# A decoder layer on one core: the 24 gate columns move from strips beside the first projection into the value projection

## The chip, the cores and the metric

The kernel runs on one NeuronCore of a Trainium2 chip. The metric is the device time of one execution in microseconds (us), the median over the runs. One execution is profiled as well; all rows below are of that execution. The core has a matrix engine (TensorE, PE in the rows, with its weight loads as PEld), a vector engine (DVE), a scalar engine (ACT), GpSimd (POOL) and queues for transfers (DMA), which SyncE (SP) issues.

## The reference

One decoder layer over 512 tokens of width 1024, everything in float32. A single input projection makes all the operands of two token mixers, among them three gates for each of eight attention heads, 24 columns in all:

```
h = x @ w_in + b_in
(q_a, kv_a, g_nsa, z_a, q_b, f_b, i_b, z_b, gm_a, gm_b) = split(h)
gates = sigmoid(g_nsa)          # 8 heads x 3 branches = 24 columns
o_a = gates[0]*o_cmp + gates[1]*o_slc + gates[2]*o_win
o_b = hgrn2(q_b, f_b, i_b); o_b = o_b * rsqrt(mean(o_b^2)+eps) * g
y = sigmoid(gm_a)*((o_a*silu(z_a)) @ Wa) + sigmoid(gm_b)*((o_b*silu(z_b)) @ Wb)
out = layer_norm(alpha*x + y @ w_out)
```

Mixer A is sparse attention with a compressed, a selected and a window branch; mixer B is a gated linear recurrence in chunks of 64 tokens.

## The kernel before

Every float32 operand of a large product is split into a high part in a reduced format and the rest (`split2`: a cast on ACT, then a subtraction on DVE), and a product is three matmuls: high by high, high by low, low by high. The input is held transposed, as eight tiles of 128 channels by 512 tokens (`xh[kt]`, `xl[kt]`, `kt` from 0 to 7).

The PE's work is one long list in program order, and so are the transfers that SP issues. First comes the projection to the forget gates `f`, a loop over `kt` in which each step does 12 matmuls into four PSUM tiles (pools `pso` and `pss`). At `kt` 3 and 7 this loop also does the gates: four unsplit float32 matmuls each, with 32 columns of weights `wgs`, whose results go to the four strips of 32 partitions of one tile `gps` (pool `pst`). ACT copies it with the bias to the tile `graw`: channels lie in partitions there, tokens along the row, and the four strips are partial sums.

Then come the projections to `q` of mixer B, the four token blocks of `proj_i` (tokens in partitions, 512 columns, 24 matmuls a block), each closed by a DVE addition of the bias (line 275), and a sequence of weight tiles of 1024 columns, which `load` brings in and `split` splits two tiles ahead. Between them a cooperative scheduler (`weave`) places pieces of other work at fixed points: it starts generators, each of which does a piece at every tick. The gates are one of these, `gates()`, started ahead of the third block of `proj_i`: four transposes of `graw` on PE, a DVE sum over the four strips, and the sigmoid with an Exp on ACT and three small DVE steps, on a tile `gat` of 128 by 128.

`proj_v` is the projection to the values, with tokens in partitions and 256 columns. Its two weight tiles `v0` and `v1` hold four `kt` each, one token block takes 24 matmuls, and after each block DVE adds the bias (line 295), ACT casts and DVE subtracts into `vv`. Behind it on PE stand the sums of squares for the norm of mixer B (`hgrn_norm`, eight records with the operand `ones`). The norm goes on through DVE line 431, ACT lines 435 and 436, sixteen small transfers on SP, and POOL line 448. Tiles of one pool share its buffers in turn, so a new tile waits for the last reader of the one that had its place before: three buffers each for the weight tiles `wraw`, `whi`, `wlo`, 67 for the general pool `t2`.

Of the kernel before, what the change touches and what calls it, by code (L numbers as in the profile page):

```python
# [18 lines left out]
P = 128  # L19
KT = DM // P  # L20
# [17 lines left out]
           "ga0 gb0 ga1 gb1 ga2 gb2 ga3 gb3 ga4 gb4 ga5 gb5 ga6 gb6 ga7 gb7").split()  # L38
M_INDEX = {n: i for i, n in enumerate(M_TILES)}
NB = 4 + len(M_TILES)  # L40


BRANCH = [("b", 0), ("b", 2), ("a", 0), ("b", 4), ("a", 2), ("b", 6), ("a", 4), ("a", 6)]
# [12 lines left out]
O_NG = O_LB + 8  # L56
O_PEK = O_NG + 4
O_PEV = O_PEK + 16
O_GB = O_PEV + 16
O_END = O_GB + 1  # L60


K_ID, K_TRI, K_CM, K_RV, K_SM, K_COS, K_SIN, K_MASK, K_END = (
# [29 lines left out]


@with_exitstack
def layer_kernel(ctx: ExitStack, tc: tile.TileContext, xT, xn, w0, wi, wg, wf, small, brow, consts,
                 w1, w2, wbr, wout, lng, lnb, out):
    nc = tc.nc
    V, A, G = nc.vector, nc.scalar, nc.gpsimd
# [10 lines left out]
    def dma(o, i):  # L110
        tc.keep_in_program_order(nc.sync.dma_start(o, i))  # L111
# [10 lines left out]
    def T2(n=512, dt=F32):  # L122
        return t2.tile([P, n], dt, name="t2", tag="t2")
# [10 lines left out]
    def PT():  # L134
        return pst.tile([P, 512], F32, name="pst", tag="pst")
# [10 lines left out]
    def split2(src, dst_hi, dst_lo):  # L146
        A.copy(dst_hi, src)  # L147
        V.tensor_tensor(dst_lo, src, dst_hi.bitcast(F32), ALU.subtract)  # L148
# [10 lines left out]
        T.matmul(warm[:, 0:128], zero, zero, start=True, stop=True)  # L159
    sml = cst.tile([P, O_END], F32, name="sml")  # L160
    con = cst.tile([P, K_SM], F32, name="con")
    wgs = T2(256)
    xs, xh, xl = [], [], []
    fps = [PO(), PO(), PS(), PS()]
    gps = PT()
    for kt in range(KT):
        xr, wr = first if kt == 0 else (T2(), T2())
        dma(xr, xT[:, kt])
        if kt:
            dma(wr, w0[kt])  # L170
        if kt == 1:
            dma(wgs, wg)
        if kt == 4:
            dma(sml, small)
        h, l, wh, wl = T2(dt=F32R), T2(dt=F32R), T2(dt=F32R), T2(dt=F32R)
        xh.append(h)
        xl.append(l)
        A.copy(h, xr)
        V.tensor_copy(wh, wr)
        V.tensor_tensor(l, xr, h.bitcast(F32), ALU.subtract)  # L180
        V.tensor_tensor(wl, wr, wh.bitcast(F32), ALU.subtract)
        xs.append(xr)
        for a, b in ((wh, h), (wh, l), (wl, h)):
            for m in range(4):
                T.matmul(fps[m], a[:, 128 * m:128 * m + 128], b, start=kt == 0 and a is wh and b is h,
                         stop=kt == KT - 1 and a is wl)
        if kt == 3 or kt == 7:
            for k in range(kt - 3, kt + 1):
                q = k % 4
                T.matmul(gps[32 * q:32 * q + 32], wgs[:, 32 * k:32 * k + 32], xs[k], start=k < 4, stop=k >= 4)  # L190


    order = M_TILES + ["br%s%d" % b for b in BRANCH]
# [27 lines left out]

    ones = cst.tile([P, 32], F32, name="ones")
    G.memset(ones, 1.0 / 128.0)
    epst = cst.tile([P, 1], F32, name="epst")
    G.memset(epst, EPS)
    hbias = cst.tile([P, NB], F32, name="hbias")
    V.tensor_scalar(hbias, sml[:, 0:NB], 0.5, None, ALU.mult)
    attn_sb = [T2() for _ in range(4)]
    for t in attn_sb:
# [6 lines left out]
    G.memset(kcB, 0.0)  # L236
    G.memset(vcB, 0.0)
    split(0)
    graw = T2()
    A.activation(graw, gps, AF.Identity, bias=sml[:, O_GB:O_GB + 1])  # L240
    sig_f = []
    for m in range(4):
        s = T2()
# [21 lines left out]
    def proj_i(tt):  # L265
# [9 lines left out]
        tc.keep_in_program_order(V.tensor_tensor(v, ps, bri, ALU.add))  # L275
        vi.append(v)

    def proj_v():
        i = M_INDEX["v0"]
        load(i + 3)  # L280
        split(i + 2)
        load(i + 4)
        for tt in range(4):
            c = slice(128 * tt, 128 * tt + 128)
            ps = PA()
            for kt in range(KT):
                if kt % 4 == 0:
                    weave.tick()
                hi, lo = parts[i + kt // 4]
                n = slice(256 * (kt % 4), 256 * (kt % 4) + 256)  # L290
                T.matmul(ps[:, 0:256], xh[kt][:, c], hi[:, n], start=kt == 0, stop=False)
                T.matmul(ps[:, 0:256], xh[kt][:, c], lo[:, n], start=False, stop=False)
                T.matmul(ps[:, 0:256], xl[kt][:, c], hi[:, n], start=False, stop=kt == KT - 1)
            v = T2(256)
            tc.keep_in_program_order(V.tensor_tensor(v, ps[:, 0:256], brv, ALU.add))
            vd = vv[:, tt].rearrange("p b (g c) -> p b g c", c=64)
            v4 = v.rearrange("p (b g c) -> p b g c", b=2, c=64)
            split2(v4, vd[:, :, 0:4:3], vd[:, :, 1:3])
            vts.append(vv[:, tt])
        split(i + 3)  # L300

    def silu_tile(name):
# [211 lines left out]
                    A.copy(dst, ps[r:r + 32, 0:64])  # L514
        ready.add("cmp")

    gat = cst.tile([P, 4, 32], F32, name="gat")
    gv = gat[:, :, 0:24].rearrange("p i (h b) -> p i h b", b=3)

    def gates():  # L520
        ps = transpose4(graw)
        gflat = gat.rearrange("p i c -> p (i c)")
        tc.keep_in_program_order(
            V.tensor_reduce(gat, ps.rearrange("p (i q c) -> p i c q", i=4, q=4), AX.X, ALU.add))
        A.activation(gflat, gflat, AF.Exp, scale=-1.0)
        V.tensor_scalar(gflat, gflat, 1.0, 2.0, ALU.add, ALU.mult)
        V.reciprocal(gflat, gflat)
        V.tensor_tensor(gv[:, :, :, 0], gv[:, :, :, 0], rvalid.unsqueeze(2).to_broadcast([P, 4, 8]), ALU.mult)
        yield 1


    def rope(raw):
# [38 lines left out]
    def cmp_probs(c):  # L571
        while "cmp" not in ready:
            yield 1
        ps = PS()
        for m in range(2):
            for i in range(4):
                T.matmul(ps[:, 128 * i + 64 * m:128 * i + 64 * m + 64],
                         qraw[2 * c + m][:, 128 * i:128 * i + 128], kcB, start=True, stop=True)
            if m == 0:
                yield 1  # L580
        s = T2()
        s4 = s.rearrange("p (i h n) -> p i h n", i=4, n=32)
        s3 = s.rearrange("p (x n) -> p x n", n=32)
        mx = SM(16, "mx")
        V.tensor_tensor(s4, ps.rearrange("p (i h n) -> p i h n", i=4, n=32),
                        cmask.unsqueeze(2).to_broadcast([P, 4, 4, 32]), ALU.add)
        V.tensor_reduce(mx, s3, AX.X, ALU.max)
        V.tensor_tensor(s3, s3, mx.unsqueeze(2).to_broadcast([P, 16, 32]), ALU.subtract)
        A.activation(s, s, AF.Exp, scale=0.125)
        yield D["p0"]  # L590
        V.tensor_reduce(mx, s3, AX.X, ALU.add)
# [12 lines left out]
    probs, pv_at = {}, [0]  # L604

    def attn_scores():
        while not {"keys0", "keys1"} <= ready or len(QAB) < 4:
            yield 1
        for u, (i, brs) in enumerate(units):
            while u - pv_at[0] > 1:  # L610
# [104 lines left out]


    vi, vts, wis = [], [], []
    bri, brv = T2(), T2(256)
    dma(bri, brow[:, 0:512].to_broadcast([P, 512]))
    dma(brv, brow[:, 512:768].to_broadcast([P, 256]))  # L720
    qs = []
    for m in range(4):
        for kt in (2 * m, 2 * m + 1):
# [34 lines left out]
        weave.start(queries(m, qraw[m]))  # L758

    for t in range(4):  # L760
        if t == 2:
            weave.start(gates())
        weave.start(hgrn(t), D["h0"])
        proj_i(t)
    for name in SEQ:
        if name[1:] == "cmp":
            cmp_tile("kv".index(name[0]), name)
            if name[0] == "v":
                weave.start(cmp_kv())
# [24 lines left out]
        zs[name] = z  # L794
# [181 lines left out]
```

## Time and profile before

| | before |
|---|---|
| median of 3 runs | 444.57 us (444.48 to 445.08) |
| the profiled execution | 445.41 us |
| its span in the profile | 443.6 us |
| granted PE clock, mean | 0.995 of full speed |
| PE busy | 434.1 us, 98% |
| DVE busy | 299.6 us, 68% |
| ACT busy | 228.2 us, 51% |
| POOL busy | 13.6 us, 3% |

The span is what the profiler saw between the first and the last instruction; the time of an execution is longer by what lies around it, 1.8 us here. A share of busy time is a mean over the whole span, and says nothing of one stage.

### The profile page before, as it was taken

What the parts mean: (1) busy time and instruction counts of PE and PEld (TensorE: products, weight loads), DVE (VectorE), ACT (ScalarE), POOL (GpSimd) and SP (SyncE); (2) the same over time, 40 slices, a digit from 0 to 9 for tenths busy, and PEclk for the clock granted to TensorE, in tenths of its full rate; (3) what the DMA queues carried; (4) which work ended last, traced back from release to release, by engine and by line L of the source; (5) the groups of instructions that cost most, each with busy time, mean ns of one, the idle gap of its engine ahead of it and who ended that gap; (6) DMA issues with size and microseconds to landing.
All of it is one profiled execution on the core that took longest, in us unless ns stands there. A gap on an engine that the chain in (4) does not pass through costs nothing.

```text
span 443.6 us, 6069 instructions
## 1 busy us (share of the span) xinstructions
PE 434.1 (98%) x2217; PEld 361.5 (81%) x2217; DVE 299.6 (68%) x598; ACT 228.2 (51%) x442; POOL 13.6 (3%) x24
## 2 busy tenths in 40 slices
PE   9999999999999999999999999999999999999993
PEld 7778878888898888887888888888888888888883
DVE  5906569995987439975665667676755598876554
ACT  3435534632456526579774677687955444344000
POOL 2000000000000120000000010001001100000000
PEclk9999999999999999999999999999999999999998
DMA  8983600232350273321121112111223362163111
GB/s 292 392 332 111 231 0 2 71 89 61 85 171 1 61 217 106 140 96 49 57 86 47 47 49 96 49 47 47 78 85 125 110 210 108 49 210 120 50 47 47
DMA packets 20445, 47.39 MB, mean 107 GB/s; under 512 B 2880, under 2 KB 3904, under 8 KB 20416
## 3 DMA queue, kind: packets, MB, share of 16 engines
q1 hardware_dynamic: 20272, 46.75, 31.3%
q8 instruction: 17, 0.28, 0.3%
q10 hardware_dynamic: 144, 0.26, 0.2%
q14 instruction: 12, 0.10, 0.1%
HBM read 41.76 MB, written 2.10 MB: 99 GB/s over the span
## 4 chain that ended last, share of the span: by engine, by line
PE 90%; DVE 2%; SPq 2%; ACT 2%; DMA 2%; issue 1%; POOL 0%; DVEq 0%; POOLq 0%; ACTq 0%
PE pa L104 56%; PE pss L104 19%; PE pso L104 10%; PE pst L108 5%; SPq L111 2%; PE pst L104 1%; DMA wraw<-in_wf_dram 1%; ACT whi L147 1%; DVE wlo L148 1%; DMA t<-t 0%; POOL t L448 0%; ACT t L564 0%; DVE t L891 0%; DVE t L893 0%; DVE t L450 0%
## 5 line engine op out<-in xcount | busy, mean ns | idle before, releaser
L104 PE MATMUL pa<-t,whi 128*128 128x512 f32 x640 | 203.5, 399 | 0.0
L104 PEld LDWEIGHTS pa<-t,whi 128*128 128x128 f32 x640 | 116.8, 188 | 25.9 <-issue 3.9
L104 PE MATMUL pa<-t,wlo 128*128 128x512 f32 x320 | 125.2, 391 | 0.0
L148 DVE TENSOR_TENSOR wlo<-wraw,whi 128x1024 fp32r<-128x1024 f32 x46 | 56.6, 1235 | 25.9 <-ACT whi L147 25.9
L104 PEld LDWEIGHTS pa<-t,wlo 128*128 128x128 f32 x320 | 60.1, 188 | 13.3
L147 ACT CAST whi<-wraw 128x1024 fp32r<-128x1024 f32 x46 | 48.1, 1046 | 36.8 <-PE pa L104 13.4
L104 PE MATMUL pss<-t,t 128*128 128x512 f32 (+5 forms) x296 | 48.4, 318 | 0.0
L104 PE MATMUL pa<-t,t 128*128 128x512 f32 x192 | 44.3, 390 | 0.8 <-DVE t L275 0.8
L104 PEld LDWEIGHTS pss<-t,t 128*128 128x128 f32 (+1 forms) x296 | 38.3, 172 | 6.8 <-issue 1.4
L632 ACT ACTIVATE t<-t,sm_mn 128x512 f32<-128x512 f32 (+3 forms) x64 | 35.8, 560 | 14.6 <-DVE sm_mn L629 13.6
L104 PEld LDWEIGHTS pa<-t,t 128*128 128x128 f32 x192 | 36.0, 188 | 8.4 <-DVE t L275 1.0
L629 DVE CUSTOM_DVE_ANT_0 t<-pss,t 128x512 f32<-128x512 f32 (+3 forms) x64 | 30.1, 487 | 16.9 <-PE pss L104 16.8
L148 DVE TENSOR_TENSOR t<-pst,t 128x512 fp32r<-128x512 f32 x40 | 27.5, 689 | 15.7 <-ACT t L147 15.7
L148 DVE TENSOR_TENSOR t<-t,t 128x512 fp32r<-128x512 f32 x36 | 23.6, 687 | 16.5 <-ACT t L147 16.4
L147 ACT CAST t<-pst 128x512 fp32r<-128x512 f32 x40 | 23.1, 580 | 17.6 <-PE pst L108 17.5
L147 ACT CAST t<-t 128x512 fp32r<-128x512 f32 x36 | 20.6, 620 | 17.4 <-DVE t L841 15.4
L108 PE MATMUL pst<-con,t 128*128 128x128 f32 x185 | 28.0, 272 | 0.0
L108 PEld LDWEIGHTS pst<-con,t 128*128 128x128 f32 x185 | 22.9, 141 | 4.3
L104 PE MATMUL pso<-t,vv 128*128 128x512 f32 x80 | 22.9, 408 | 0.0
L104 PE MATMUL pso<-t,t 128*128 128x128 f32 (+1 forms) x104 | 22.1, 332 | 0.0
L104 PE MATMUL pss<-t,whi 128*128 128x512 f32 x64 | 19.7, 389 | 0.0
L643 ACT ACTIVATE t<-t,sm_dn 128x512 f32<-128x512 f32 (+3 forms) x32 | 16.6, 557 | 4.3 <-DVE sm_dn L638 4.2
(154 smaller groups left out, 489.9 us busy)
## 6 DMA issues: line engine op xcount, KB each, us to landing
wraw<-in_wf_dram SPq DMA_DIRECT2D x38, 512.0 KB, 3.5
wraw<-in_wbr_dram SPq DMA_DIRECT2D x8, 512.0 KB, 3.6
t<-in_wout_dram SPq DMA_DIRECT2D x16, 256.0 KB, 3.9
t<-in_w_dram SPq DMA_DIRECT2D x15, 256.0 KB, 6.1
t<-t SPq DMA_DIRECT2D x48, 64.0 KB, 2.0
t<-in_xT_dram SPq DMA_DIRECT2D x8, 256.0 KB, 4.8
t<-in_wi_dram SPq DMA_DIRECT2D x8, 256.0 KB, 6.4
t<-in_xn_dram SPq DMA_DIRECT2D x8, 256.0 KB, 6.0
```

The source lines that it names most:

```text
L104: return tc.keep_in_program_order(nc.tensor.matmul(*a, **k))
L108: return tc.keep_in_program_order(nc.tensor.transpose(*a, **k))
L111: tc.keep_in_program_order(nc.sync.dma_start(o, i))
L147: A.copy(dst_hi, src)
L148: V.tensor_tensor(dst_lo, src, dst_hi.bitcast(F32), ALU.subtract)
L629: V.tensor_tensor_reduce(out=p[:, c], in0=ps[:, c], in1=amask[:, 512 - n:512], op0=ALU.add, op1=ALU.min, scale=-0.125, scalar=3.0e38, accu ...
L632: A.activation(p[:, c], p[:, c], AF.Exp, bias=mn[:, k], scale=-1.0, accum_out=den[:, k])
L643: A.mul(ts[m][:, c], ts[m][:, c], den[:, k])
```

## The change

The gate columns become columns 256 to 279 of the value projection. The two strip groups, the weight tile `wgs` and its transfer, the tile `graw` with its ACT copy, and the four transposes with the sum over strips go. The 96 matmuls of `proj_v` have 280 columns in place of 256. A weight tile still has 1024 columns; at 280 columns (pitch 320) it holds three `kt` instead of four, so `v0` and `v1` hold `kt` 0 to 5, and `kt` 6 and 7 come in two tiles of their own (`wv`, 128 by 280), which `split_vtail` loads and splits ahead of the first `q` tile. After each token block POOL copies 24 columns to `gat` (now 128 by 96), and `gates()` runs after the fourth block, without a transpose. The users of the gates wait for the mark "gates".

```diff
-        if kt == 1:
-            dma(wgs, wg)
...
-        if kt == 3 or kt == 7:
-            for k in range(kt - 3, kt + 1):
-                q = k % 4
-                T.matmul(gps[32 * q:32 * q + 32], wgs[:, 32 * k:32 * k + 32], xs[k], start=k < 4, stop=k >= 4)
...
-    graw = T2()
-    A.activation(graw, gps, AF.Identity, bias=sml[:, O_GB:O_GB + 1])
...
+    def split_vtail():
+        for k in range(2):
+            raw, hi, lo = T2(NV), T2(NV, F32R), T2(NV, F32R)
+            dma(raw, wv[k])
+            split2(raw, hi, lo)
+            vtail.append((hi, lo))
...
-                hi, lo = parts[i + kt // 4]
-                n = slice(256 * (kt % 4), 256 * (kt % 4) + 256)
-                T.matmul(ps[:, 0:256], xh[kt][:, c], hi[:, n], start=kt == 0, stop=False)
...
+                if kt < 6:
+                    n = slice(PV * (kt % 3), PV * (kt % 3) + NV)
+                    hi, lo = (t[:, n] for t in parts[i + kt // 3])
+                else:
+                    hi, lo = vtail[kt - 6]
+                T.matmul(ps[:, 0:NV], xh[kt][:, c], hi, start=kt == 0, stop=False)
...
+            G.tensor_copy(gat[:, tt], v[:, 256:NV])
             vts.append(vv[:, tt])
+        gates()
         split(i + 3)
...
     def gates():
-        ps = transpose4(graw)
         gflat = gat.rearrange("p i c -> p (i c)")
-        tc.keep_in_program_order(
-            V.tensor_reduce(gat, ps.rearrange("p (i q c) -> p i c q", i=4, q=4), AX.X, ALU.add))
         A.activation(gflat, gflat, AF.Exp, scale=-1.0)
         V.tensor_scalar(gflat, gflat, 1.0, 2.0, ALU.add, ALU.mult)
         V.reciprocal(gflat, gflat)
         V.tensor_tensor(gv[:, :, :, 0], gv[:, :, :, 0], rvalid.unsqueeze(2).to_broadcast([P, 4, 8]), ALU.mult)
-        yield 1
+        ready.add("gates")
...
-        if t == 2:
-            weave.start(gates())
...
+            if m == 0:
+                split_vtail()
```

On PE, in the `f` loop at `kt` 3, before (the `t_` numbers are buffers of the general pool):

```order
L104 MATMUL pso<-t_177,t_180 128x512 x2
L104 MATMUL pss<-t_177,t_180 128x512 x2
L104 MATMUL pst<-t_79,t_97 32x512
L104 MATMUL pst<-t_124,t_97 32x512
L104 MATMUL pst<-t_149,t_97 32x512
L104 MATMUL pst<-t_173,t_97 32x512
L104 MATMUL pso<-t_206,t_208 128x512 x2
```

The same place after the change:

```order
L104 MATMUL pso<-t_175,t_176 128x512 x2
L104 MATMUL pss<-t_175,t_176 128x512 x2
L104 MATMUL pso<-t_174,t_177 128x512 x2
L104 MATMUL pss<-t_174,t_177 128x512 x2
L104 MATMUL pso<-t_199,t_201 128x512 x2
L104 MATMUL pss<-t_199,t_201 128x512 x2
```

The four strips are gone and nothing has taken their place; the next `kt` follows at once.

On PE, the last matmuls of a token block of `proj_v` before (`whi`, `wlo` are the split weight tile; `v1` is used to the end):

```order
L104 MATMUL pa<-whi,t_254 128x256
L104 MATMUL pa<-wlo,t_254 128x256
L104 MATMUL pa<-whi,t_255 128x256
L104 MATMUL pa<-whi,t_278 128x256
L104 MATMUL pa<-wlo,t_278 128x256
L104 MATMUL pa<-whi,t_279 128x256
```

And after the change:

```order
L104 MATMUL pa<-whi,t_223 128x280
L104 MATMUL pa<-wlo,t_223 128x280
L104 MATMUL pa<-whi,t_224 128x280
L104 MATMUL pa<-t_1068,t_247 128x280
L104 MATMUL pa<-t_1069,t_247 128x280
L104 MATMUL pa<-t_1068,t_248 128x280
L104 MATMUL pa<-t_1074,t_271 128x280
L104 MATMUL pa<-t_1075,t_271 128x280
L104 MATMUL pa<-t_1074,t_272 128x280
```

The last six matmuls of a block read the two tiles of their own (`t_1068` to `t_1075`), so `v1` has its last reader six matmuls ahead of the end, and `v0` fifteen ahead in place of twelve.

On DVE, around the end of `proj_v` before (line 295 is the bias, line 148 a subtraction of `split2`, line 431 the first step of the norm, with `pss` the sums of squares):

```order
L295 TENSOR_TENSOR t_1416<-pa,t_364 128x256
L148 TENSOR_TENSOR wlo<-wraw,whi 128x1024
L148 TENSOR_TENSOR vv<-t_1416,vv 128x2x128
L295 TENSOR_TENSOR t_1445<-pa,t_364 128x256
L148 TENSOR_TENSOR wlo<-wraw,whi 128x1024
L431 TENSOR_SCALAR t_1465<-pss 128x512
L148 TENSOR_TENSOR vv<-t_1445,vv 128x2x128
L148 TENSOR_TENSOR wlo<-wraw,whi 128x1024
```

And after (line 435 is the former line 431, lines 527 to 529 the gates):

```order
L297 TENSOR_TENSOR t_1407<-pa,t_351 128x280
L148 TENSOR_TENSOR wlo<-wraw,whi 128x1024
L148 TENSOR_TENSOR vv<-t_1407,vv 128x2x128
L297 TENSOR_TENSOR t_1437<-pa,t_351 128x280
L148 TENSOR_TENSOR wlo<-wraw,whi 128x1024
L148 TENSOR_TENSOR vv<-t_1437,vv 128x2x128
L527 TENSOR_SCALAR gat<-gat 128x96
L435 TENSOR_SCALAR t_1462<-pss 128x512
L528 RECIPROCAL gat<-gat 128x96
L529 TENSOR_TENSOR gat<-gat,con 128x32
L148 TENSOR_TENSOR wlo<-wraw,whi 128x1024
```

The last subtraction into `vv` and the first step of the gates now stand ahead of the norm's first step on DVE. On ACT, correspondingly, the Exp of the gates stands between the last cast into `vv` and line 435 (now 439). From the sums of squares on, PE's own order is the same in both kernels.

## Rows read from the trace of the kernel before

**Rows 1.** The page: busy time, share and instructions of each engine.
```profile
PE 434.1 (98%) x2217; PEld 361.5 (81%) x2217; DVE 299.6 (68%) x598; ACT 228.2 (51%) x442; POOL 13.6 (3%) x24
```

**Rows 2.** PE's waits, two of four: total us, times, longest.
```profile
...
PE pa L104 <- DVE t L275: 0.8, 1, 0.8
...
PE pss L104 <- ACT t L312: 0.2, 1, 0.2
```

**Rows 3.** Windows: us; busy PE, PEld, DVE, ACT, POOL; clock; DMA share; GB/s.
```profile
...
64.00:126.00 62.00, 62.00 (x386) 52.20 (x386) 54.38 (x106) 23.78 (x44) 0.52 (x4) 1.00 0.24 73
...
```

**Rows 4.** PE's timeline around the first strips: start, us, instruction.
```profile
16.05 0.61 PE L104 MATMUL pss<-t,t 128*128 128x512 f32 x2
16.59 1.06 PE L104 MATMUL pst<-t,t 128*32 128x512 f32 x8
...
19.54 0.39 PE L104 MATMUL pso<-t,t 128*128 128x512 f32 x1
```

**Rows 5.** PE's timeline around the second strips.
```profile
28.16 0.61 PE L104 MATMUL pss<-t,t 128*128 128x512 f32 x2
28.70 1.07 PE L104 MATMUL pst<-t,t 128*32 128x512 f32 x8
...
30.96 0.40 PE L104 MATMUL pa<-t,wlo 128*128 128x512 f32 x1
```

**Rows 6.** DVE's timeline: the last split of the `f` loop's operands.
```profile
17.16 0.69 DVE L181 TENSOR_TENSOR t<-t,t 128x512 fp32r<-128x512 f32 x1
```

**Rows 7.** PE's timeline through the four blocks of `proj_i`.
```profile
51.59 11.05 PE L104 MATMUL pa<-t,t 128*128 128x512 f32 x48
62.48 0.60 PE L108 MATMUL pst<-con,t 128*128 128x128 f32 x4
63.87 11.15 PE L104 MATMUL pa<-t,t 128*128 128x512 f32 x48 [0.78 <-DVE t L275]
74.86 0.39 PE L104 MATMUL pa<-t,whi 128*128 128x512 f32 x1
```

**Rows 8.** DVE's timeline there: the bias of `proj_i`, a gate step.
```profile
63.12 1.29 DVE L275 TENSOR_TENSOR t<-pa,t 128x512 f32<-128x512 f32 x2 [3.88 <-PE pst L108]
...
68.41 0.22 DVE L526 TENSOR_SCALAR gat<-gat 128x128 f32<-128x128 f32 x1
```

**Rows 9.** PE's timeline in the last token block of `proj_v`.
```profile
139.13 0.28 PE L104 MATMUL pa<-wlo,t 128*128 128x256 f32 x1
...
141.77 0.28 PE L104 MATMUL pa<-whi,t 128*128 128x256 f32 x1
```

**Rows 10.** ACT's timeline around the end of `proj_v`.
```profile
140.69 1.05 ACT L147 CAST whi<-wraw 128x1024 fp32r<-128x1024 f32 x1 [0.99 <-ACT t L564]
...
142.13 1.05 ACT L147 CAST whi<-wraw 128x1024 fp32r<-128x1024 f32 x1
143.19 1.28 ACT L144 ACT_TABLE_LOAD   x1
144.49 0.41 ACT L147 CAST vv<-t 128x256 fp32r<-128x256 f32 x1
```

**Rows 11.** DVE's timeline: the first step of the norm.
```profile
144.72 0.68 DVE L431 TENSOR_SCALAR t<-pss 128x512 f32<-128x512 f32 x1
```

**Rows 12.** The chain that ended last, where it comes back to PE.
```profile
172.04 1.10 PE pss L104 x8
```

**Rows 13.** POOL's and DVE's timelines where both read SBUF, and DVE alone.
```profile
150.71 1.28 POOL L448 TENSOR_TENSOR t<-t,t 128x512 f32<-128x512 f32 x1 [65.17 <-DMA t<-t]
150.92 1.63 DVE L793 SCALAR_TENSOR_TENSOR t<-t,t 128x512 f32<-128x512 f32 x1
165.96 0.69 DVE L793 SCALAR_TENSOR_TENSOR t<-t,t 128x512 f32<-128x512 f32 x1
```

**Rows 14.** PE's timeline: the next longer matmul of the attention scores.
```profile
253.16 0.33 PE L104 MATMUL pss<-kh,t 128*128 128x384 f32 x1
253.33 0.34 PE L104 MATMUL pss<-kl,t 128*128 128x384 f32 x1
```

More of the change, by code (lines that the diff above doesn't have):

```diff
@@ L40 @@
 NB = 4 + len(M_TILES)
+NV, PV = 256 + 24, 320
 BRANCH = [("b", 0), ("b", 2), ("a", 0), ("b", 4), ("a", 2), ("b", 6), ("a", 4), ("a", 6)]
@@ L58 @@
 O_PEV = O_PEK + 16
-O_GB = O_PEV + 16
-O_END = O_GB + 1
+O_END = O_PEV + 16
 K_ID, K_TRI, K_CM, K_RV, K_SM, K_COS, K_SIN, K_MASK, K_END = (
@@ L95, in layer_kernel @@
 @with_exitstack
-def layer_kernel(ctx: ExitStack, tc: tile.TileContext, xT, xn, w0, wi, wg, wf, small, brow, consts,
+def layer_kernel(ctx: ExitStack, tc: tile.TileContext, xT, xn, w0, wi, wf, wv, small, brow, consts,
                  w1, w2, wbr, wout, lng, lnb, out):
@@ L161, in layer_kernel @@
     con = cst.tile([P, K_SM], F32, name="con")
-    wgs = T2(256)
-    xs, xh, xl = [], [], []
+    xh, xl = [], []
     fps = [PO(), PO(), PS(), PS()]
-    gps = PT()
     for kt in range(KT):
@@ L181, in layer_kernel @@
         V.tensor_tensor(wl, wr, wh.bitcast(F32), ALU.subtract)
-        xs.append(xr)
         for a, b in ((wh, h), (wh, l), (wl, h)):
@@ L223, in layer_kernel @@
     G.memset(ones, 1.0 / 128.0)
+    hbias = cst.tile([P, NB], F32, name="hbias")
     epst = cst.tile([P, 1], F32, name="epst")
     G.memset(epst, EPS)
-    hbias = cst.tile([P, NB], F32, name="hbias")
     V.tensor_scalar(hbias, sml[:, 0:NB], 0.5, None, ALU.mult)
@@ L276, in proj_i @@
         vi.append(v)
+    vtail = []
+    def split_vtail():
[4 more added lines that the diff above has]
+            vtail.append((hi, lo))
     def proj_v():
@@ L288, in proj_v @@
                     weave.tick()
-                hi, lo = parts[i + kt // 4]
-                n = slice(256 * (kt % 4), 256 * (kt % 4) + 256)
-                T.matmul(ps[:, 0:256], xh[kt][:, c], hi[:, n], start=kt == 0, stop=False)
[L292 to L295, printed above, removed]
+                if kt < 6:
[4 more added lines that the diff above has]
+                T.matmul(ps[:, 0:NV], xh[kt][:, c], hi, start=kt == 0, stop=False)
+                T.matmul(ps[:, 0:NV], xh[kt][:, c], lo, start=False, stop=False)
+                T.matmul(ps[:, 0:NV], xl[kt][:, c], hi, start=False, stop=kt == KT - 1)
+            v = T2(NV)
+            tc.keep_in_program_order(V.tensor_tensor(v, ps[:, 0:NV], brv, ALU.add))
             vd = vv[:, tt].rearrange("p b (g c) -> p b g c", c=64)
-            v4 = v.rearrange("p (b g c) -> p b g c", b=2, c=64)
+            v4 = v[:, 0:256].rearrange("p (b g c) -> p b g c", b=2, c=64)
             split2(v4, vd[:, :, 0:4:3], vd[:, :, 1:3])
+            G.tensor_copy(gat[:, tt], v[:, 256:NV])
             vts.append(vv[:, tt])
+        gates()
         split(i + 3)
@@ L515, in cmp_kv @@
         ready.add("cmp")
-    gat = cst.tile([P, 4, 32], F32, name="gat")
-    gv = gat[:, :, 0:24].rearrange("p i (h b) -> p i h b", b=3)
+    gat = cst.tile([P, 4, 24], F32, name="gat")
+    gv = gat.rearrange("p i (h b) -> p i h b", b=3)
     def gates():
-        ps = transpose4(graw)
         gflat = gat.rearrange("p i c -> p (i c)")
-        tc.keep_in_program_order(
-            V.tensor_reduce(gat, ps.rearrange("p (i q c) -> p i c q", i=4, q=4), AX.X, ALU.add))
         A.activation(gflat, gflat, AF.Exp, scale=-1.0)
@@ L590, in cmp_probs @@
         yield D["p0"]
+        while "gates" not in ready:
+            yield 1
         V.tensor_reduce(mx, s3, AX.X, ALU.add)
@@ L606, in attn_scores @@
     def attn_scores():
-        while not {"keys0", "keys1"} <= ready or len(QAB) < 4:
+        while not {"keys0", "keys1", "gates"} <= ready or len(QAB) < 4:
             yield 1
@@ L717, in layer_kernel @@
     vi, vts, wis = [], [], []
-    bri, brv = T2(), T2(256)
+    bri, brv = T2(), T2(NV)
     dma(bri, brow[:, 0:512].to_broadcast([P, 512]))
-    dma(brv, brow[:, 512:768].to_broadcast([P, 256]))
+    dma(brv, brow[:, 512:512 + NV].to_broadcast([P, NV]))
     qs = []
@@ L929 @@
     small = np.zeros((128, O_END), f32)
-    wg = np.zeros((128, 8, 32), f32)
-    wg[:, :, :24] = w[:, C_G:C_G + 24].reshape(8, 128, 24).transpose(1, 0, 2)
-    small[:24, O_GB] = b[C_G:C_G + 24]
     for m in range(4):
@@ L938 @@
         small[:, 4 + m] = b[c]
-    cv = np.r_[C_KV + 384:C_KV + 512, C_KV + 640:C_KV + 768]
-    wv = w[:, cv].reshape(2, 4, 128, 256).transpose(0, 2, 1, 3)
+    cv = np.r_[C_KV + 384:C_KV + 512, C_KV + 640:C_KV + 768, C_G:C_G + 24]
+    wv = w[:, cv].reshape(8, 128, NV)
     for j in range(2):
-        wf[M_INDEX["v%d" % j]] = wv[j].reshape(128, 8, 128)
+        t = wf[M_INDEX["v%d" % j]].reshape(128, 1024)
+        for k in range(3):
+            t[:, PV * k:PV * k + NV] = wv[3 * j + k]
     brow = np.concatenate([b[C_I:C_I + 512], b[cv]])[None]
@@ L958 @@
     arrays_in = dict(
-        xT=xT, xn=x, w0=w0, wi=wi, wg=wg.reshape(128, 256),
-        wf=wf.reshape(len(M_TILES), 128, 1024), small=small, brow=brow, consts=_constants(),
+        xT=xT, xn=x, w0=w0, wi=wi,
+        wf=wf.reshape(len(M_TILES), 128, 1024), wv=wv[6:], small=small, brow=brow, consts=_constants(),
         w1=w1, w2=w2, wbr=wbr, wout=a["w_out"][0].reshape(8, 128, 1024),
```

## Prediction
> **What bounds the kernel now.** I read the busy shares first, then PE's waits, then PE's own timeline, and last the chain that ended last. PE is busy for 434.1 of the 443.6 us [rows 1]. Its waits are few and short, 0.8 and 0.2 us for those that this change could touch [rows 2], and in the stretch from 64 to 126 us it is busy for 62.00 of 62 us [rows 3]. So PE's list of instructions is the time, and a change is priced by what it takes out of that list and adds to it. DVE is busy for 54.38 us of the same 62 [rows 3]: too little slack to be called free, too much to be the bound.
>
> There is one place where PE is only just supplied. The chain leaves PE near the end of the value projection, goes through the norm of mixer B, its sixteen transfers and a weight tile behind them on the same queue, and comes back to PE at 172.04 [rows 12], where PE waits 0.2 us [rows 2]. There the chain sets the time: what makes it later against the value projection adds to the end, one for one.
>
> **The unit.** 48 matmuls of 512 columns begin at 51.59, and the next instruction at 62.48 [rows 7]: 10.89 / 48 = 0.227 us each. For 256 columns the starts at 139.13 and 141.77 lie 22 matmuls apart [rows 9]: 0.120 us. The slope between them is 0.107 / 256, or 0.42 ns a column.
>
> **What goes.** First strips: from 16.05 to 19.54 PE does ten ordinary matmuls (five rows of two) beside the strips [rows 4]. Ten cost 2.27 us, the stretch is 3.49: the strips cost **1.22**. Second strips: from 28.16 to 30.96 there are seven ordinary ones, 1.59 of 2.80 us: **1.21** [rows 5]. Can PE use that time? The operands of the whole `f` loop are split by 17.85 us [rows 6], while the loop runs to 28.70, so nothing upstream is late.
>
> Transposes: between 62.48 and 74.86 lie 48 matmuls of `proj_i`, 10.89 us of 12.38, so the transposes cost **1.49** [rows 7]. Of this 0.78 is PE's wait for line 275 [rows 7, 8]. DVE had stood idle 3.88 us before that line until the transposes had been read [rows 8], because the output tile of the first block takes the buffer of `graw`. Without `graw` the addition can run as soon as the first block is done, half of the 48 matmuls after 51.59, near 57; the third block wants its PSUM buffer only at 62.48. So the wait goes with the transposes and nothing else comes in its place. The ACT copy, the strip sum and the transfer of `wgs` were on no chain, and count nothing. Sum: 1.22 + 1.21 + 1.49 = 3.92 us.
>
> **What is added on PE.** 96 matmuls get 24 columns: 24 x 0.42 = 10 ns each, **0.96** us together. The trace has no matmul of 280 columns. From below the cost is nothing, if matmuls this short are paced by something other than columns; from above, the next length in the trace, 384 columns, starts every 0.17 us [rows 14], 0.05 more than for 256, or 4.8. The two lengths of one kind lie on a line through 384 as well (0.120 + 128 x 0.00042 = 0.173), so I take the line.
>
> **What is added off PE.** The two tiles of 128 by 280 cost two transfers of 143 KB, two casts and two subtractions, of about 0.4 us each (the cast of 128 by 256 took 0.41 [rows 10]). They are ordered before the first `q` tile, far ahead of the value projection, whose last token block alone begins near 139. I cost them at nothing; the cover is DVE's slack of 7.6 us in 64 to 126 [rows 3], and DVE loses the strip sum and three gate steps in the same stretch. Without cover, two subtractions would be 0.8 us.
>
> **What moves: the chain after the value projection.** Let E be the end of its last matmul, 142.05 before [rows 9]. The norm's first step began at E + 2.67 [rows 11]. After, ACT's first weight cast waits for the last reader of `v0`, 15 matmuls of 0.13 us before E, not 12 of 0.12: it can begin at E - 1.87 where it began at E - 1.36 [rows 10]. The second waits for `v1`, free six matmuls before E; it follows the first and a cast of 0.41, so it ends near E + 0.65 where it ended at E + 1.13. The table load of 1.28 follows, and the last cast into `vv` of 0.41 [rows 10] ends near E + 2.36. Until here the order gains half a microsecond. But now the Exp of the gates (I take 0.3, a cast of that kind being 0.41) and the gates' first DVE step of 0.22 [rows 8] stand ahead of the norm's first step: some E + 2.95, with the handing over between engines. The chain is 0.3 later. The users of the gates stand behind them on DVE's own list and wait for nothing new; on POOL the norm's line 448, which began at 150.71 [rows 13], stands behind the four copies and is not held by them.
>
> To this comes the POOL copy of the last block. POOL and DVE hold each other up in this trace: a DVE step of 0.69 us took 1.63 when it began 0.21 after a POOL step of 1.28 [rows 13], ending 0.56 after POOL. The copy of 24 columns falls on the subtraction of a weight tile. From below it costs nothing, from above the whole 1.28 of a POOL step on 512 columns. With a twentieth of the columns it is nearer to the lower end; I take 0.1. Together **0.4** on the chain.
>
> The Trainium skill ("SBUF — State Buffer", "SBUF: two separate sides") says that DVE with two SBUF inputs and a GpSimd operation that reads SBUF take turns on one port pair, an exclusive lock held for the whole instruction. By that rule the trace agrees: the 1.63 us are the rest of POOL's 1.28 and then DVE's own 0.6. The rule speaks against a POOL copy at this place, and by it the copy costs its full length, whatever that is; the rows above bound it.
>
> **The sum.** -3.92 + 0.96 + 0.4 = -2.56 us. The profiled execution took 445.41 us, 1.8 more than its span and 0.84 above the median, which I take as an offset that stays; so 445.41 becomes 442.85, and the median 444.57 becomes **442.0** us.
>
> **The rivals.** *The chain is later than I think.* If the POOL copy costs the full 1.28 [rows 13] on top of the 0.3, PE stalls some 1.6 us near 172, and the gain is 3.92 - 0.96 - 1.6 = 1.4: 443.2 us. For it: the chain has no slack there [rows 2]. Against: 24 columns are few.
>
> *The gain is given back to another wait.* PE would reach the stretch from 64 us nearly 4 us sooner, and there DVE is 88% busy [rows 3]. If DVE's chain sets the pace there, PE waits 2 to 3 us in that stretch, and the kernel ends within 0.9 us of before. Against: PE has no wait there now, and DVE gains too, by 3.88 us of idle time that goes [rows 8] and by the gate steps.
>
> *The wider matmul costs more than its columns.* If 280 columns pace like 384 at 0.17 us [rows 14], 96 of them cost the 4.8 us worked out above, more than all that is saved: -3.92 + 4.8 + 0.4 = +1.3, or 445.9 us, slower. It decides from (3.92 - 0.4) / 96 = 37 ns more for one matmul. Against it: three lengths on one line.
>
> *The gain is larger.* If the chain is not later at all, since the weight casts come earlier, and the wider matmuls hide part of their columns behind weight loads, up to 3.9 us are gained: 440.7 to 441.3.
>
> **How the numbers follow.** I give the forecast 0.63 (its own range, with 0 to 0.9 on the chain and 0.7 to 1.1 for the columns, is 441.2 to 442.6), the later chain 0.13, the gain given back 0.10, the wider matmul 0.06, the larger gain 0.08. A measurement of this kernel can tell about 0.2%, 0.9 us, from no change. Faster by more: 0.63 + 0.13 + 0.08 = 0.84; the same 0.10; slower 0.06. The range takes in the forecast, the later chain and half of the larger gain, and leaves out some 0.2: 441.1 to 443.6 us.
>
> **What would show it.** On PE: no `pst` rows of 32 columns; the stretches that held them shorter by 1.2 us each; 96 matmuls in `proj_i` from the first to the last in 21.8 us, with no wait for the bias line; and `proj_v` rows with 280 columns every 0.130 us. The norm's first DVE step at some 2.95 us behind the last of them, and at the chain's return PE's wait 0.6 in place of 0.2. Wrong I would be if the 280-column pace is above 0.14, if the norm's first step comes 4 us behind the values, or if PE's list of waits shows a new DVE releaser between 64 and 126 us.

## The result and the profile after

The changed kernel took 442.68 us (median of 6, 441.79 to 443.20), the kernel before beside it 445.08 (444.48 to 445.33). The ratio is 0.9947, with a 95% interval from 0.9933 to 0.9961: 2.4 us faster, where 2.6 was forecast (442.0 us in a range of 441.1 to 443.6). The profiled execution took 442.84 us, its span is 441.0 where before had 443.6.

The page of the kernel after, busy time and share of each engine (beside [rows 1]), and then PE's waits (total us, times, longest; beside [rows 2]):

```profile
PE 432.4 (98%) x2197; PEld 362.4 (82%) x2197; DVE 297.8 (68%) x599; ACT 228.1 (52%) x443; POOL 16.6 (4%) x28
```

```profile
PE pso L104 <- DVE t L156: 1.1, 1, 1.1
PE pst L104 <- DVE kcB L508: 0.3, 1, 0.3
PE pss L104 <- ACT t L316: 0.2, 1, 0.2
```

The wait for the bias of `proj_i` (0.8 in [rows 2]) is gone, and no new releaser has come. PE is still busy for 98% of the span. PE's timeline after, in four places (start, us, instruction): the end of the `f` loop, the whole of `proj_i`, the last block of `proj_v`, and the return of the norm's chain:

```profile
27.37 0.61 PE L104 MATMUL pss<-t,t 128*128 128x512 f32 x2
27.82 0.62 PE L104 MATMUL pa<-t,whi 128*128 128x512 f32 x2
...
49.58 21.92 PE L104 MATMUL pa<-t,t 128*128 128x512 f32 x96
71.34 0.62 PE L104 MATMUL pa<-t,whi 128*128 128x512 f32 x2
...
136.47 0.29 PE L104 MATMUL pa<-wlo,t 128*128 128x280 f32 x1
...
138.38 0.29 PE L104 MATMUL pa<-wlo,t 128*128 128x280 f32 x1
...
138.64 0.93 PE L104 MATMUL pa<-t,t 128*128 128x280 f32 x6
139.50 1.06 PE L104 MATMUL pss<-t,ones 128*32 128x512 f32 x8
...
169.55 1.10 PE L104 MATMUL pss<-kcB,t 128*128 128x64 f32 x8 [0.15 <-ACT t L316]
```

The last `f` matmuls at 27.37 are followed by the first weight tile 0.45 us later; before, 1.00 us of strips stood there (28.70 in [rows 5] to 29.70, where the weight tile began):

```profile
29.70 0.73 PE L104 MATMUL pa<-t,whi 128*128 128x512 f32 x2
```

After, all 96 matmuls of `proj_i` form one row: 21.76 us from start to start, 0.227 each, with no gap where the transposes were. Fifteen matmuls of 280 columns lie between 136.47 and 138.38: 0.127 us each. The chain comes back at 169.55, and PE waits 0.15.

Between four marks on PE's timeline the two kernels compare as follows. A is the first matmul of the first weight tile behind the `f` loop, B the first behind `proj_i`, C the first of the value projection, D the sums of squares behind it; each time is a difference of starts in the timeline, in us. The other rows are the runs of the next section.

| run | start to A | A to B | B to C | C to D | D to end | span |
|---|---|---|---|---|---|---|
| before | 29.70 | 45.16 | 51.12 | 16.00 | 301.6 | 443.6 |
| after | 27.82 | 43.52 | 51.12 | 17.04 | 301.5 | 441.0 |
| x1, no strips | 26.91 | 45.02 | 51.12 | 15.99 | 301.3 | 440.3 |
| x2, own tile, 66 buffers | 29.97 | 44.12 | 52.99 | 15.99 | 301.2 | 444.3 |
| x3, 256 columns | 28.05 | 43.52 | 51.12 | 16.60 | 301.9 | 441.2 |
| x4, 320 columns | 27.91 | 43.51 | 51.12 | 18.58 | 301.1 | 442.2 |
| x5, after again | 27.41 | 43.51 | 51.12 | 17.03 | 301.2 | 440.3 |
| x6, own tile, 67 buffers | 30.07 | 44.12 | 51.12 | 15.99 | 301.5 | 442.8 |
| x7, late norm | 27.62 | 43.52 | 51.11 | 17.04 | 302.8 | 442.1 |
| x8, tail split twice | 27.78 | 43.52 | 51.12 | 17.55 | 301.5 | 441.5 |
| x9, gates behind | 27.71 | 43.52 | 51.12 | 17.02 | 301.3 | 440.7 |
| x10, tail on GpSimd | 27.94 | 43.52 | 51.12 | 17.04 | 301.4 | 441.0 |
| x11, both | 26.94 | 43.52 | 51.12 | 17.04 | 301.2 | 439.8 |

From A to B the change saves 1.64 us (some 0.13 of it is the slower start behind the second strips: the weight tile's first three matmuls, from 29.70 to 30.50, take 0.80 us before and 0.68 after), from C to D it costs 1.04, and everything between repeats to 0.01 us. Only the first column and the tail scatter. Up to A the change saved 1.88 us where two groups of strips are 2.43; the two profiles differ in the very first matmuls of the `f` loop, before any strip. Rows of PE's timeline there, first before, then after:

```profile
5.28 0.95 PE L104 MATMUL pso<-t,t 128*128 128x512 f32 x2
6.07 0.63 PE L104 MATMUL pss<-t,t 128*128 128x512 f32 x2
6.53 0.61 PE L104 MATMUL pso<-t,t 128*128 128x512 f32 x2
6.98 0.62 PE L104 MATMUL pss<-t,t 128*128 128x512 f32 x2
```

```profile
5.05 1.20 PE L104 MATMUL pso<-t,t 128*128 128x512 f32 x2
6.04 1.05 PE L104 MATMUL pss<-t,t 128*128 128x512 f32 x2
6.89 0.66 PE L104 MATMUL pso<-t,t 128*128 128x512 f32 x2
7.39 0.62 PE L104 MATMUL pss<-t,t 128*128 128x512 f32 x2
```

Before began 0.23 us later but needed 0.79 us for its first pair and 0.46 from then on; after needed 0.99, 0.85 and 0.50 for three pairs. So after is 0.41 us behind at the fourth pair, and this hides part of what the strips gave. The next section shows that it does not belong to the change.

### The profile page after: what moved, and what is told of

The parts are those of the page before. It is cut to its first block, busy times and chain, and to the rows that moved or that the text cites. A ratio compares the mean times of both kernels' runs of the same rounds, so it can differ in the third digit from the quotient of the medians.

```text
span 441.0 us, 6036 instructions
## 1 busy us (share of the span) xinstructions
PE 432.4 (98%) x2197; PEld 362.4 (82%) x2197; DVE 297.8 (68%) x599; ACT 228.1 (52%) x443; POOL 16.6 (4%) x28
## 4 chain that ended last, share of the span: by engine, by line
PE 91%; SPq 2%; DVE 2%; ACT 1%; DMA 1%; issue 1%; POOL 0%; DVEq 0%; ACTq 0%
PE pa L104 56%; PE pss L104 19%; PE pso L104 10%; PE pst L108 4%; SPq L111 2%; DMA wraw<-in_wf_dram 1%; PE pst L104 1%; ACT whi L147 1%; DVE wlo L148 0%; POOL gat L301 0%; DVE t L894 0%; DVE t L896 0%; DVE t L454 0%; DVEq L975 0%; ACT t L439 0%
## 5 line engine op out<-in xcount | busy, mean ns | idle before, releaser
L104 PE MATMUL pa<-t,t 128*128 128x512 f32 (+1 forms) x216 | 47.7, 378 | 0.0
L104 PEld LDWEIGHTS pa<-t,t 128*128 128x128 f32 x216 | 39.4, 188 | 7.5
L148 DVE TENSOR_TENSOR t<-t,t 128x512 fp32r<-128x512 f32 (+1 forms) x38 | 24.3, 673 | 12.4 <-ACT t L147 12.3
L147 ACT CAST t<-t 128x512 fp32r<-128x512 f32 (+1 forms) x38 | 21.4, 608 | 17.4 <-DVE t L844 15.4
```

The costliest lines, as they stand in the source:

```text
L104: return tc.keep_in_program_order(nc.tensor.matmul(*a, **k))
```

## The experiments

**x1: the strips alone.** In the kernel before:

```diff
-    gps = PT()
...
-        if kt == 3 or kt == 7:
-            for k in range(kt - 3, kt + 1):
-                q = k % 4
-                T.matmul(gps[32 * q:32 * q + 32], wgs[:, 32 * k:32 * k + 32], xs[k], start=k < 4, stop=k >= 4)
...
-    A.activation(graw, gps, AF.Identity, bias=sml[:, O_GB:O_GB + 1])
+    A.activation(graw[:, 0:256], wgs, AF.Identity, bias=sml[:, O_GB:O_GB + 1])
+    A.activation(graw[:, 256:512], wgs, AF.Identity, bias=sml[:, O_GB:O_GB + 1])
```

> The kernel before with both strip groups left out and nothing else moved; the transposed gate tile is filled from the gate weights, so the gates of the reference are not computed. By the forecast's first two terms PE loses 1.22 + 1.21 = 2.43 us and nothing upstream is late: 2.4 us faster than before, a ratio near 0.9945, and PE's f loop ends 2.4 us sooner. Rival: the profile after the change reached the end of the f loop only 2.0 us sooner, since its first eight matmuls were slower; if that belongs to leaving the strips or their weights out, this kernel too gains only 2.0 us (0.9955) and its first matmuls are slow.

Measured: 442.09 us against 445.10, a ratio of 0.9935 (0.9923 to 0.9948), 3.0 us faster. In the profile A comes at 26.91, 2.79 earlier than before, and this time the first matmuls run at full pace from the start (PE's timeline of x1):

```profile
5.03 0.70 PE L104 MATMUL pso<-t,t 128*128 128x512 f32 x2
5.57 0.62 PE L104 MATMUL pss<-t,t 128*128 128x512 f32 x2
6.03 0.63 PE L104 MATMUL pso<-t,t 128*128 128x512 f32 x2
```

From here the pairs follow every 0.46 us. Counted from the fourth pair (6.49 here, 6.98 before) to B, which leaves the start out, x1 saves 2.44 us, so the strips are worth their 2.43, and the rest is the start. The rival, that leaving the strips out makes the start slow, falls.

**x5: the changed kernel once more**, with no edit.

> The changed kernel once more, unaltered. In its first profile the first four matmuls of the f loop took 1.8 us where before took 1.25, and this cost 0.44 us of the gain. If that varies from run to run, this profile may show the loop's end some 0.5 us earlier (near 27.3 us after the start) and the medians scatter by as much; if it belongs to the change, the loop ends again near 27.8 us. Time 442 to 443 us.

Measured: 442.21 us against 445.27, a ratio of 0.9929 (0.9917 to 0.9942), 3.1 us faster. A comes at 27.41, between the two. Over the nine profiles of programs that have the same PE instructions up to A (after, x3 to x5, x7 to x11) A lies from 26.94 to 28.05 us. So the first microseconds differ by up to 1.1 us from execution to execution, and the 0.41 us lost in the first profile are that. What differs is TensorE's clock. The trace's first record of the granted clock, at full speed, begins at 5.80 us in before, at 6.95 in after, at 6.03 in x5 and at 4.67 in x1. Ahead of it matmuls of 512 columns start 0.43 us apart (a pair took 0.85 in the rows of after above), behind it 0.23. The last section has this for all the profiles. Outside the start the change is worth 2.43 + 1.51 - 1.04 = 2.9 us in the profiles. The two medians, 2.4 and 3.1, lie on both sides of it.

**x2: the channel tile in a place of its own**, in the kernel before:

```diff
-    t2 = ctx.enter_context(tc.tile_pool(name="t2", bufs=67))
+    t2 = ctx.enter_context(tc.tile_pool(name="t2", bufs=66))
...
-    graw = T2()
+    graw = cst.tile([P, 512], F32, name="graw")
```

> The kernel before with the gates' channel tile in a place of its own (the general pool has 66 buffers in place of 67, so that it fits). By the third term DVE's line 275 no longer waits for the transposes, and PE's 0.78 us of waiting goes: 0.8 us faster, a ratio near 0.998, with the four transposes still 0.6 to 0.7 us of PE. Rival: the first block's output then waits for the next buffer in turn, and PE waits as before: 1.000.

Measured: 446.04 us against 445.10, a ratio of 1.0020 (1.0011 to 1.0029), slower. The wait for line 275 is gone, and from A to B PE is 1.04 us shorter. Then this comes (DVE's timeline, and PE's; L358 writes a tile of the general pool):

```profile
69.31 0.69 DVE L358 TENSOR_TENSOR t<-sm_cm,t 128x512 f32<-128x512 f32 x1 [2.01 <-PE pa L104]
```

```profile
81.82 1.38 PE L104 MATMUL pss<-t,t 128*64 128x64 f32 x13 [1.79 <-DVE t L376]
```

With one buffer fewer, line 358's output has another predecessor, one that PE still reads; DVE idles 2.01 us in a stretch where it was busy for 88% before [rows 3], and PE waits 1.79 us for it later. It shows how little room DVE has there, but says nothing of the change's third term by itself.

**x6: the same with the pool's turn kept**, in the kernel before (`asum` is not written until the attention's end; the call of `T2()` leaves one buffer unused):

```diff
-    graw = T2()
+    T2()
+    graw = asum[:, 0]
```

> The kernel before with the gates' channel tile in a place that is free until the attention's end, and the general pool's turn kept as it was (67 buffers, one left unused in its place), so that no other tile gets another predecessor. By the third term PE's 0.78 us of waiting for line 275 goes and nothing comes in its place: 0.8 to 1.0 us faster, a ratio near 0.998. Rival, from the run with 66 buffers: a wait of about that size comes back later (there 1.8 us in front of the first chunk products), and the time is that of before or longer.

Measured: 444.01 us against 445.27, a ratio of 0.9975 (0.9964 to 0.9985): 1.3 us faster by the medians, 1.1 by the ratio. PE's timeline at the transposes:

```profile
62.85 0.60 PE L108 MATMUL pst<-con,asum 128*128 128x128 f32 x4
63.20 11.15 PE L104 MATMUL pa<-t,t 128*128 128x512 f32 x48
74.19 0.62 PE L104 MATMUL pa<-t,whi 128*128 128x512 f32 x2
```

48 matmuls and the transposes take 11.34 us where they took 12.38 [rows 7]: 1.04 less. Of this 0.78 is the wait; the other 0.26 is that PE, where it needn't wait, starts the next matmul ahead of the last transpose's end (63.20, where 62.85 + 0.60 is 63.45). No wait takes its place (B to C 51.12, C to D 15.99). So the better part of the third term, which was a buffer's turn, could be had without moving the gates at all; the transposes proper are 0.45 us.

**x3 and x4: the price of columns**, in the changed kernel. x3 has 256 columns (the gates come from value columns then), x4 has 320, with zeros in the 40 more:

```diff
-                T.matmul(ps[:, 0:NV], xh[kt][:, c], hi, start=kt == 0, stop=False)
+                T.matmul(ps[:, 0:256], xh[kt][:, c], hi[:, 0:256], start=kt == 0, stop=False)
...
-            G.tensor_copy(gat[:, tt], v[:, 256:NV])
+            G.tensor_copy(gat[:, tt], v[:, 0:24])
```

```diff
-            raw, hi, lo = T2(NV), T2(NV, F32R), T2(NV, F32R)
+            raw, hi, lo = T2(PV), T2(PV, F32R), T2(PV, F32R)
...
-                    n = slice(PV * (kt % 3), PV * (kt % 3) + NV)
+                    n = slice(PV * (kt % 3), PV * (kt % 3) + PV)
...
-                T.matmul(ps[:, 0:NV], xh[kt][:, c], hi, start=kt == 0, stop=False)
+                T.matmul(ps[:, 0:PV], xh[kt][:, c], hi, start=kt == 0, stop=False)
...
```

> The changed kernel with the value matmuls and their bias at 256 columns, all else kept; the gates are made from value columns, so they are not the reference's. By the fourth term 96 x 10 ns = 0.96 us goes: 1.0 us faster than the changed kernel, about 441.7 us, a ratio to before near 0.9925. Rival: the 1.04 us that PE lost in that stretch is something else (the two tiles of their own, breaks in the row of matmuls), and the time stays that of the changed kernel, 0.9947.

> The changed kernel with the value matmuls at 320 columns, the 40 more holding zeros that are not read (the two tiles of their own are as wide). By the price of 0.42 ns a column 96 x 40 x 0.42 = 1.6 us slower than the changed kernel, about 444.3 us, a ratio to before near 0.998. Rival: matmuls are priced in steps, so that 280 and 320 cost the same: 0.9947.

Measured: x3 442.04 us, 0.9927 (0.9914 to 0.9941); x4 443.14 us, 0.9956 (0.9943 to 0.9968). The medians fit the forecast for x3 and fall short of it for x4, but their intervals are over 1 us wide, and the stages tell more. x4's value stretch is 1.54 us longer than that of the changed kernel, near the forecast of 1.6: the price goes by columns, not by steps. Two things cancel in the 1.54. The matmuls start every 0.147 us (15 of them between the two rows of x4's PE timeline below), some 1.8 us more for the 96 than at 280 columns; and 0.28 us that the changed kernel loses in front of its third token block are not lost here.

```profile
137.66 0.31 PE L104 MATMUL pa<-wlo,t 128*128 128x320 f32 x1
...
139.86 0.31 PE L104 MATMUL pa<-wlo,t 128*128 128x320 f32 x1
```

x3's stretch is only 0.44 us shorter, and its waits say why (PE's waits in x3):

```profile
PE pss L104 <- ACT t L316: 0.5, 1, 0.5
PE pa L104 <- DVE t L297: 0.4, 1, 0.4
```

PE is ready for the third token block before DVE has read the first one's PSUM (line 297, 0.4 us), and waits 0.5 in place of 0.15 where the chain returns. So narrower matmuls would give back most of what they save: around the value projection PE and DVE are nearly even after the change.

**x7: the norm later**, in the changed kernel:

```diff
         V.tensor_scalar(rs, pm, EPS, None, ALU.add)
+        for _ in range(2):
+            V.tensor_scalar(rs, rs, 0.0, None, ALU.add)
```

> The changed kernel with two more DVE steps (adding zero, 128 by 512, some 0.4 to 0.7 us each) behind the norm's first one, so that the norm's chain is about 1 us later and nothing else changes. By the claim that the chain sets the time where it comes back to PE, PE's wait there grows from 0.15 to about 1.1 us and the kernel is 1.0 us slower than the changed one, a ratio to before near 0.997. Rival: the transfers or the weight tile behind them absorb it, as they seem to have absorbed the 0.1 us that the gates' steps added: no change, 0.9947.

Measured: 443.60 us against 445.27, 0.9958 (0.9945 to 0.9972), 1.4 us slower than x5, measured beside it. The norm's first ACT step (line 441 here) began 4.99 us behind D, in the changed kernel 3.58 (143.08, line 439). The weight tile's transfer followed at 17.92 behind D in place of 16.72 (the chain that ended last, first in the changed kernel, then in x7):

```profile
156.22 4.92 DMA wraw<-in_wf_dram
```

```profile
157.21 4.98 DMA wraw<-in_wf_dram
```

PE's waits are (in x7):

```profile
PE pss L104 <- ACT t L316: 0.8, 1, 0.8
...
PE pa L104 <- ACT t L797: 0.3, 1, 0.3
```

From D to the end it is 1.3 us longer than after. Of 1.41 us of lateness 1.20 reach the transfer and about as much the end: the chain does set the time, and some 0.2 us are absorbed on the way.

**x8: the tail split twice**, in the changed kernel:

```diff
             split2(raw, hi, lo)
+            split2(raw, hi, lo)
             vtail.append((hi, lo))
```

> The changed kernel with the two tiles of their own split twice (two more casts on ACT and two more subtractions on DVE, 0.4 us each, with the same result). By the forecast this work lies under DVE's slack and the time does not change (0.9947). Rival: DVE, which reaches the value projection only 2.4 us earlier than before where PE is 3.5 us earlier, is what PE waits for there, and 0.8 us more of DVE work before it makes the kernel 0.4 to 0.8 us slower (0.9957 to 0.9965), with PE waiting for line 297.

Measured: 442.73 us against 445.27, 0.9945 (0.9933 to 0.9958), 0.5 us above x5. The value stretch is 0.51 us longer, with a wait of 0.5 for the bias of a block (line 298 here). But it isn't the added work that is late. DVE's timeline in x8, and then in the changed kernel:

```profile
112.50 2.11 DVE L552 TENSOR_TENSOR t<-t,t 64x512 f32<-64x512 f32 x3
115.53 0.69 DVE L148 TENSOR_TENSOR kl<-t,kh 128x512 fp32r<-128x512 f32 x1 [0.92 <-ACT kh L147]
116.14 1.22 DVE L148 TENSOR_TENSOR wlo<-wraw,whi 128x1024 fp32r<-128x1024 f32 x1
```

```profile
115.05 1.22 DVE L148 TENSOR_TENSOR wlo<-wraw,whi 128x1024 fp32r<-128x1024 f32 x1 [1.73 <-ACT whi L147]
116.19 1.28 DVE L148 TENSOR_TENSOR kl<-t,kh 128x512 fp32r<-128x512 f32 x2
```

After the added work DVE idles in both, 0.92 and 1.73 us, so the work itself is covered. What changed is the order of the next two steps. The cast that `wlo` needs ended at 114.98 on ACT in x8 and at 115.02 in the changed kernel, but with `kl` first DVE waits for another cast and begins 0.48 us later. From there to the bias DVE's only gap of more than 0.1 us is a wait of 0.69 for ACT, and it is the same in both, so it takes nothing of this up.

**x9 to x11: the gates behind the norm, the tail's subtractions on GpSimd, and both**, in the changed kernel:

```diff
-        gates()
+        weave.start(gates(), 6)
...
+        yield 1
```

```diff
-            split2(raw, hi, lo)
+            A.copy(hi, raw)
+            G.tensor_tensor(lo, raw, hi.bitcast(F32), ALU.subtract)
```

> The changed kernel with the gates' DVE steps placed behind the norm's first step (they start as a later piece of the scheduler). If the gates' step of 0.2 us ahead of the norm is a cost on the chain, PE's wait of 0.15 us where the chain comes back goes: at most 0.15 us faster, which the medians cannot tell; the profile can. Rival, from the run with a later norm: some 0.2 us are absorbed between the norm and the weight tile, so that PE's wait stays.

> The changed kernel with the subtractions for the two tiles of their own on GpSimd, which has nothing to do there, in place of DVE. If 0.8 us of DVE work before the value projection holds it up (twice the work made the value stretch 0.5 us longer), the 0.16 us gap in front of the third token block and PE's wait at the chain's return go: 0.2 to 0.3 us faster than the changed kernel (0.9940 beside 0.9947). Rival: GpSimd and DVE hold each other up, the DVE steps beside the two GpSimd steps take longer by some 0.7 us, and the time is the same or 0.3 us longer.

> Both together: the gates behind the norm and the two subtractions on GpSimd. 0.3 us faster than the changed kernel if the two add up; if the chain only follows the value projection, the same as with the subtractions alone.

Measured: 442.46, 442.98 and 442.34 us against 445.06, ratios of 0.9941 (0.9929 to 0.9953), 0.9952 (0.9938 to 0.9966) and 0.9940 (0.9928 to 0.9952). In all three C to D stays at 17.02 to 17.04 and PE's list has no wait at the chain's return; but x5, which is the changed kernel itself, has none there either. So x9's 0.15 us cannot be told from the scatter between executions. x10 settles x8: 0.8 us of DVE work less ahead of the value projection changes nothing (C to D 17.04), and the DVE steps beside the two on GpSimd are not longer (1.23 and 0.74 us where they were 1.23 and 0.73). None of the three is measurably better than the changed kernel.

## Why the prediction was right

The sign, the size (2.56 forecast, 2.4 and 3.1 measured in two sets of runs) and the way to it hold: PE's list of instructions is the time. That the first result lies within 0.2 us of the forecast is in part luck, as the last two points below show. By its steps:

- **Strips, 1.22 and 1.21.** Right. Counted from the fourth pair of the `f` loop (6.98 before, 7.39 after) to B, which leaves the start out, the change saves 3.93 us, where strips and transposes were put at 3.92. x1 shows the strips by themselves.
- **Transposes, 1.49.** Right in size and cause: the 96 matmuls of `proj_i` now run through. x6 splits the term: 1.04 for the buffer's turn (the wait, and the overlap that it takes away), 0.45 for the transposes.
- **24 columns, 0.96.** The value stretch grew by 1.04. The columns themselves are a little cheaper than put: 0.127 against 0.120 us a matmul, 0.76 for the 96 when each is set against its like before. The other 0.28 stands at the third token block: its first matmul starts 0.16 late, right after DVE's line 297 (the block before it reaches its next matmul 0.93 us after its last row of six, another block 0.77), and the second follows it after 0.23 us where it was 0.12 before. x3 shows what stands behind the gap. The rival of a wider step is refuted by x4.
- **The chain, 0.4.** This is the term that was mis-sized: nothing of it is seen. The steps come as described, but the norm's first step lies 2.86 us behind D where it lay 2.74 (144.72 in [rows 11], D at 141.98), 0.12 later and not 0.3 to 0.4. PE's wait at the return is 0.15 where it was 0.2 [rows 2]; nine of the thirteen profiles, x5 among them, list no wait there. x7 shows that lateness of this kind reaches PE, less some 0.2 us that the way absorbs. 0.12 lies below that. Why 0.12 and not 0.3: ACT's first cast begins 1.88 us ahead of E, the end of the last value matmul (138.64 + 0.93 = 139.57), as forecast, but the prediction added up the durations of the casts, and their starts lie closer (0.95 and 0.31 us apart where they last 1.05 and 0.40, rows below). So the second weight cast ends at E + 0.42 in place of E + 0.65, and the last cast into `vv` at E + 2.14 in place of E + 2.36.
- **The POOL copy.** The clash came, but the other way round. The timelines of the changed kernel, POOL, DVE, ACT and again DVE:

```profile
138.33 0.20 POOL L301 COPY gat<-t 128x24 f32<-128x24 f32 x1 [6.03 <-DVE t L297]
140.75 1.13 POOL L301 COPY gat<-t 128x24 f32<-128x24 f32 x1 [2.22 <-DVE t L297]
```

```profile
140.61 1.21 DVE L148 TENSOR_TENSOR wlo<-wraw,whi 128x1024 fp32r<-128x1024 f32 x1
```

```profile
137.69 1.05 ACT L147 CAST whi<-wraw 128x1024 fp32r<-128x1024 f32 x1 [0.76 <-PE pa L104]
138.64 0.40 ACT L147 CAST vv<-t 128x256 fp32r<-128x256 f32 x1
138.95 1.04 ACT L147 CAST whi<-wraw 128x1024 fp32r<-128x1024 f32 x1
140.01 1.28 ACT L144 ACT_TABLE_LOAD   x1
141.30 0.41 ACT L147 CAST vv<-t 128x256 fp32r<-128x256 f32 x1
141.92 0.28 ACT L526 ACTIVATE gat<-gat 128x96 f32<-128x96 f32 x1 [0.21 <-POOL gat L301]
```

```profile
142.23 0.21 DVE L527 TENSOR_SCALAR gat<-gat 128x96 f32<-128x96 f32 x1
142.36 0.68 DVE L435 TENSOR_SCALAR t<-pss 128x512 f32<-128x512 f32 x1
```

The reader is to see that DVE's subtraction began 0.14 us ahead of the copy and took its usual 1.21 us, while the copy, 0.20 us where it runs alone, took 1.13 and ended just behind it. The Exp waited 0.21 us for the copy. The Trainium skill ("SBUF — State Buffer", "SBUF: two separate sides") has the first of two such instructions hold the ports to its end; by that the copy's 1.13 us are DVE's rest, and these rows agree with it as those before do [rows 13]: 1.07 of the 1.13 lie ahead of the subtraction's end. The prediction let the copy hold up DVE, and here DVE held up the copy. Most of that lay under a table load and a cast on ACT that had to pass anyway; 0.21 us came through, where 0.1 was put, and the earlier casts made up for it.

- **Costs put at nothing.** x10 confirms the tail's split as covered. x8 shows that the cover is not 7.6 us of slack to spend freely: behind 115 us DVE has a run of steps up to the third token block whose one gap takes nothing up, and half a microsecond of reordering there comes out on PE.
- **What the sum left out.** The first eight matmuls of the `f` loop differ by up to 1.1 us between executions with the moment at which the clock rises, which is as large as the terms argued about. The terms outside the start add up to 2.9, not 2.56, for the chain's 0.4 did not come. In the first profile the clock rose 1.15 us later than in that of before; as far as that profile stands for its six runs, this took back about what the sum had lacked.

## What to carry to other kernels

Where one engine is busy for 98% of the span, count the instructions in and out of its list and price each from the distance between starts in its own timeline; here that gave the stage sums on PE to 0.1 us. The same goes for a chain on other engines: here ACT's casts started 0.1 us closer to each other than their durations say. A stall ahead of a reused buffer can often be had back by giving the tile another place, but a pool with one buffer fewer shifts every tile's predecessor: the same idea gave 1.1 to 1.3 us one way and cost 0.9 the other. Before you argue about tenths of a microsecond, look at how far the same instructions lie apart in several profiles, and at the pace of the first matmuls: two profiles in which the clock rose at different moments differ by that alone.

## What the runs showed of the hardware

TensorE's clock at the start. In every one of the thirteen traces the first record of the granted clock, at full speed, begins somewhere from 4.04 us (x11) to 7.28 us (x3). Ahead of it a trace has no record; a view prints 1.00 for a stretch without one, so the 1.00 that it gives for 4 to 10 us in before and after says nothing. The pace does, and in each of the traces it changes at that very moment. The 512-column matmuls of the `f` loop start 0.43 us apart as long as they lie ahead of it, and 0.23 behind it. In x11 the moment falls among the 18 matmuls of 128 columns that PE does from 1.05 us on in every run, and their distance falls there from 0.21 to 0.11 us, so that their row is shorter (PE's timeline, first the changed kernel, then x11):

```profile
1.05 4.21 PE L104 MATMUL pso<-t 128*128 128x128 f32 x18 [1.05 <-DVE t L156]
```

```profile
1.05 3.69 PE L104 MATMUL pso<-t 128*128 128x128 f32 x18 [1.05 <-DVE t L156]
```

By this pace, about half, PE ran at the lower of its two levels (1.2 and 2.4 GHz) up to that moment. It accounts for the scatter of the start: take from mark A the start of the first `f` matmul, and half of the time from there to the clock's record, and the nine profiles of the changed start lie from 21.79 to 21.88 us, where A itself lies from 26.94 to 28.05; before, x2 and x6, which have the strips, lie at 24.14 to 24.15. Late operands were not the cause of the slow pairs (PE's list of waits names none there behind the first 18 matmuls, except 0.3 us in x11). Why the clock rises earlier in one execution than in another is not shown.

Matmuls of the value projection start every 0.120, 0.127 and 0.147 us at 256, 280 and 320 columns: 0.3 ns a column at first and 0.5 then, so the line through 256 and 512 is good to a few nanoseconds and not better.
